# A decoder layer on eight cores: tail split by tokens, normalisation finish on two chunks per instruction, tanh gates, fifteen shared weight units, and a new instruction order

## Chip, cores and metric

The kernel runs on one Trainium2 chip, on 8 cores. Every core runs the same program on its own sequence, without talking to the others. The metric is the time of the slowest core, in microseconds (us). Each run lists the span of every core; the time is about 1.5 us more than the slowest span.

Some executions fall into a slower state: the cores of one die, or of both, show a lower granted clock and the time grows, in these runs to between 1601 and 1876 us. Only fast runs are compared below, and every time quoted is a median of fast runs. A ratio is the mean time of one kernel's fast runs over that of the other's fast runs of the same rounds, so it is not quite the ratio of the medians that are quoted.

## The reference, cut to what matters

```python
# one layer; d_model 1024, d_ff 2816; 2064 prompt tokens + 16 single-token samples per core
x = x + 0.5 * rmsnorm(swiglu(rmsnorm(x, g1a), Wg1, Wu1, Wd1), g1b)
h = rmsnorm(x, g2a); u = h @ W_in
yA = (A_b * dwconv3(A_c * A_x)) @ W_outA
#   RG-LRU:  r = sigmoid(x Wr + br);  i = sigmoid(x Wi + bi)
#            log_a = -8 r softplus(-lambda);  a = exp(log_a)
#            h_t = a_t h_{t-1} + sqrt(1 - a_t^2) * (i_t * x_t)
yB = (gelu(B_gate) * rglru(dwconv4(B_x))) @ W_outB
x = x + rmsnorm((sigmoid(gA) * yA + sigmoid(gB) * yB) @ W_o, g2b)
x = x + 0.5 * rmsnorm(swiglu(rmsnorm(x, g3a), Wg2, Wu2, Wd2), g3b)
```

## The kernel before

A core's 2080 tokens are cut into five streams of 414 to 418 columns, and one matmul works on the columns of one stream. The weights of the layer are cut into 117 units, mostly of 512 KB in bf16. A ring of ten slots (`wring`) holds units on the chip. Streams 0 and 1 form group 0 and use each unit together; streams 2, 3 and 4 are groups 1, 2 and 3. Group 0 reads the f32 weights (`wall`) with a cast on the way and writes a bf16 copy (`wsc`), which the later groups read. So during group 0, roughly the first 700 us, a core moves the most bytes for each matmul.

`JOIN` says for how many units stream 2 joins group 0 at the start, so that a unit serves three streams and is not fetched again:

```python
GROUPS = [[0, 1], [2], [3], [4]]
NW = 10          # slots of the weight ring
JOIN = 7
...
for u in range(JOIN if g == 1 else 0, NUNITS):
    w = head[u] if g == 0 and u < HEAD else at(g, u, "weights", None, issue_unit, g, u)
    ...
    for i in members:
        work(STREAMS[i], g, u, w)
    if g == 0 and u < JOIN:
        shared.append((u, w))          # stream 2 works on these too
```

The order of the instructions on each engine is not the order of the program text. A planner runs when the kernel is built. It simulates all engines and the DMA queues with its own durations, and at each step it gives an engine the ready operation with the best priority. The priorities come from tables of numbers (`LAGS`, `STARTS`, `ENDS`, `CLASSES`) that an earlier search found for this program. On the chip each engine then follows its fixed list and waits on semaphores. First, an operation that the planner thinks is late sits late in the list, whether or not it is late on the chip. Second, any edit can move the whole order.

```python
CAST_BW = 265e3                     # the planner's DMA figures before
COPY_BW = 400e3
DMA_CAP = (0.72, 0.95)
HW_SHARE = (0.43, 0.22)
DMA_LAT = 2.4
...
lo = min(c[0] for c in cands)
pick = min((c for c in cands if c[0] <= lo + PRI_EPS), key=lambda c: (c[1], c[2]))
```

The helpers `act`, `tt`, `stt` and `scan` record one ScalarE (ACT) or VectorE (DVE) operation each. The recurrent gate of one 128-channel block took nine ACT passes, all `Exp` and `Ln`:

```python
act(r, pzr, AF.Exp, scale=-1.0, bias=dcol(0, j));  act(b, pzi, AF.Exp, scale=-1.0, bias=dcol(1, j))
act(r, r, AF.Ln, bias=1.0);                        act(r, r, AF.Exp, scale=-1.0)
act(a, r, AF.Exp, scale=dcol(2, j));               act(r, r, AF.Exp, scale=dcol(5, j))
act(r, r, AF.Ln, bias=1.0, scale=-1.0);            act(b, b, AF.Ln, bias=1.0)
stt(r, r, 0.5, b, ALU.mult, ALU.subtract);         act(r, r, AF.Exp)
tt(cb, r, cb, ALU.mult);                           scan(b, a, cb, CAR[:, j:j + 1], ...)
```
(Lengths and dependency lists are cut in this excerpt.)

The finish of a normalisation is a multiply and an add per 128-row chunk, eight chunks. For the last stream nothing is left to hide them, and every two chunks are stored:

```python
for oc in range(KC):                                   # KC = 8
    yv = O32[s][:, oc * m:(oc + 1) * m]
    tt(tv[0:m], y32[s][:, oc, 0:m], rv[0:m], ALU.mult, ...)
    tt(yv, xs_view(st, oc, o, n), tv[0:m], ALU.add, ...)
    if st.last and (oc + 1) % 2 == 0:
        events.append(store_y(st, oc - 1, oc + 1))     # one contiguous piece per partition
```

## Time and profile before

| | before |
|---|---|
| time of the four fast runs beside the changed kernel | median 1564.96 us (1563.51 to 1565.91) |
| spans of the eight cores in the profiled run | 1557.1 to 1563.7 us, mean 1561.6 |
| TensorE (PE) busy on the slowest core | 1532.3 us |
| last matmul to end of span, all cores | 13.8 to 14.2 us |

The page of the profile, on the slowest core (core 0): the span, the busy time of each engine with the number of instructions, and the group of ACT table loads (busy time, mean ns of one, and the idle time before them with its main releaser).

```profile
span 1563.7 us, 27199 instructions; the slowest of 8 cores (1557.1 to 1563.7 us)
...
PE 1532.3 (98%) x8771; PEld 847.6 (54%) x8771; DVE 813.1 (52%) x1535; ACT 771.8 (49%) x1367; POOL 247.7 (16%) x470
...
L676 ACT ACT_TABLE_LOAD x84 | 107.8, 1283 | 28.9 <-PE P L662 19.2
```

PE is the bound. A gain must come from its start, its stalls or what follows its last matmul.

The view of waits for PE between 30 and 1535 us: what PE waited for, us in total, how often, the longest.

```profile
PE P L662 <- DVE qp L680: 3.9, 2, 2.8
PE P L662 <- DVE xs L704: 2.6, 2, 2.2
PE P L662 <- DMA wring<-wsc: 1.9, 2, 1.0
...
```

With a line of 0.7 us that is left out, the waits sum to 9.1 us in 1505 us. Two are long: 2.8 us for the norm of stream 2 near 80 us, and 2.2 us near 1233 us.

The view by windows (core 0): the window and its length, then busy us and instructions of PE, weight load, DVE, ACT and POOL, then granted clock, DMA share and GB/s.

```profile
60.00:80.00 20.00, 17.39 (x99) 9.32 (x96) 7.46 (x14) 6.62 (x14) 2.21 (x5) 1.00 0.70 158
80.00:100.00 20.00, 19.79 (x103) 10.63 (x104) 8.63 (x16) 6.75 (x10) 0.79 (x2) 0.91 0.75 187
300.00:320.00 20.00, 18.94 (x107) 10.20 (x106) 18.85 (x34) 17.01 (x33) 2.14 (x4) 1.00 0.69 162
...
700.00:720.00 20.00, 20.00 (x117) 11.14 (x115) 4.09 (x7) 4.07 (x8) 2.11 (x4) 1.00 0.92 170
1220.00:1240.00 20.00, 17.79 (x92) 9.15 (x91) 15.35 (x43) 14.88 (x28) 3.17 (x6) 0.91 0.53 171
```

A full window holds about 115 matmuls. The windows at 60, 80, 300 and 1220 us are short of that. After the two long waits the mean granted clock is 0.91: in finer windows it is 0.50 for about 3.4 us after each wait and 1.00 otherwise, so such a wait costs some ten matmuls more than its own length. At 300 us DVE (18.85 of 20 us) and ACT (17.01) are nearly full as well: this is the mixer of group 0, where the two are almost as scarce as PE.

The end of the span, from the timeline (start, length, engine, operation; in brackets the idle time before it and its releaser), and then the DMA view from 1549 us on, with the median us from issue to landing at the end of the second line:

```profile
1549.56 0.34 PE L662 MATMUL P<-qp,ones 128*128 128x414 bf16 x1 [0.58 <-ACT qp L676]
...
1551.27 0.59 DVE L680 TENSOR_TENSOR fp<-hy,fp 128x414 f32<-128x414 f32 x1 [5.01 <-ACT fp L676]
...
1560.32 0.59 DVE L680 TENSOR_TENSOR big<-xs,fp 128x414 f32<-128x414 f32 x1
```

```profile
DMA packets 576, 1.70 MB, mean 113 GB/s; under 512 B 64, under 2 KB 64, under 8 KB 576
...
yout<-big SPq DMA_DIRECT2D x4, 414.0 KB, 2.5
```

After PE's last matmul, sixteen DVE operations of 0.59 us run one after another, and 2.8 us after the last of them the span ends. Of the 576 packets, 512 are pieces of 3312 bytes (two chunks of 414 floats); each 414 KB store lands in 2.5 us.

### The profile page before, as it was taken

To read this page: it belongs to the slowest core of one execution; us is meant where nothing else is said; L and a number is where in the kernel's file an instruction comes from. 1 tells how busy PE (TensorE), PEld (TensorE's weight loads), DVE (VectorE), ACT (ScalarE), POOL (GpSimd) and SP (SyncE) were. 2 spreads that over 40 slices of the span, in tenths; PEclk is the share of its full clock that TensorE was granted. 3 is DMA by queue.
4 is the path that set the end of the run, shared out by engine and by line. 5 is a ranking of instruction groups with operands and counts; after the bars stand their busy time and mean duration, and the time that the engine had idled before them with its cause. 6 is when DMAs were issued, how large, how long until landed. Compare 5 with 4: busy or idle time off the path is not lost.

```text
span 1563.7 us, 27199 instructions; the slowest of 8 cores (1557.1 to 1563.7 us)
## 1 busy us (share of the span) xinstructions
PE 1532.3 (98%) x8771; PEld 847.6 (54%) x8771; DVE 813.1 (52%) x1535; ACT 771.8 (49%) x1367; POOL 247.7 (16%) x470
## 2 busy tenths in 40 slices
PE   8999999999999999999999999999999999999996
PEld 5555555555555555555555555555555555555553
DVE  3232108988787467722127452356567887661143
ACT  3221136788877567411154332446575678451222
POOL 1001111011111111011111122222221111112220
PEclk9999999999999999999999999999999999999998
DMA  9889767766877775898766776655575555545653
GB/s 192 227 193 205 155 159 179 200 146 190 203 162 191 201 201 145 200 203 188 180 178 189 249 247 202 198 181 172 183 254 202 163 174 186 205 170 181 199 185 106
DMA packets 81002, 294.88 MB, mean 189 GB/s; under 512 B 9696, under 2 KB 9824, under 8 KB 80864
## 3 DMA queue, kind: packets, MB, share of 16 engines
q0 software_dynamic: 60704, 223.12, 56.2%
q1 hardware_dynamic: 20160, 70.02, 11.9%
q8 instruction: 74, 1.21, 0.3%
q14 instruction: 64, 0.52, 0.1%
HBM read 284.76 MB, written 64.45 MB: 223 GB/s over the span
## 4 chain that ended last, share of the span: by engine, by line
PE 93%; DVE 3%; DMA 2%; issue 1%; ACT 1%; DVEq 0%; POOL 0%; SPq 0%; ACTq 0%; POOLq 0%
PE P L662 93%; DMA xs<-xin 1%; DMA wring<-wsc 1%; DVE fp L694 1%; DVE fp L680 1%; ACT fp L676 0%; DVE big L680 0%; ACT L676 0%; DVE xs L704 0%; DVE fp L699 0%; DVE fp L688 0%; DVEq L1143 0%; DVE qp L680 0%; ACT qp L676 0%; DVE xs L680 0%
## 5 line engine op out<-in xcount | busy, mean ns | idle before, releaser
L662 PE MATMUL P<-hy,wring 128*128 128x414 bf16 (+4 forms) x6080 | 1101.3, 339 | 5.7 <-DVE xs L704 2.2
L662 PEld LDWEIGHTS P<-hy,wring 128*128 128x128 bf16 x6080 | 591.0, 97 | 487.8 <-issue 14.4
L676 ACT ACTIVATE fp<-P 128x414 f32<-128x414 f32 (+4 forms) x529 | 267.7, 516 | 625.1 <-PE P L662 613.2
L662 PE MATMUL P<-big,wring 128*128 128x414 bf16 (+3 forms) x2400 | 442.8, 338 | 0.3 <-DVE xs L704 0.3
L680 DVE TENSOR_TENSOR big<-P,fp 128x414 bf16<-128x414 f32 (+3 forms) x260 | 151.2, 588 | 403.7 <-PE P L662 379.6
L662 PEld LDWEIGHTS P<-big,wring 128*128 128x128 bf16 x2400 | 233.2, 97 | 189.3 <-issue 1.0
L734 POOL DMA_DIRECT2D wring<-wsc x344 | 182.9, 532 | 802.5 <-PE P L662 786.1
L680 DVE TENSOR_TENSOR fp<-fp 128x414 f32<-128x414 f32 (+3 forms) x215 | 122.5, 572 | 131.2 <-ACT fp L676 124.3
L734 POOL DMA_DIRECT2D wring<-wall x117 | 62.0, 533 | 470.8 <-PE P L662 446.5
L676 ACT ACTIVATE fp<-fp 128x418 f32<-128x418 f32 (+2 forms) x230 | 121.1, 546 | 13.3 <-DVE fp L694 4.0
L676 ACT ACT_TABLE_LOAD x84 | 107.8, 1283 | 28.9 <-PE P L662 19.2
L694 DVE SCALAR_TENSOR_TENSOR fp<-P,par_sb,fp 128x418 f32<-128x418 f32 (+3 forms) x120 | 77.4, 646 | 24.9 <-ACT fp L676 16.9
L694 DVE SCALAR_TENSOR_TENSOR hy<-xs,par_sb,fp 128x414 bf16<-128x414 f32 (+3 forms) x120 | 69.1, 646 | 21.0 <-ACT fp L676 21.0
L694 DVE SCALAR_TENSOR_TENSOR fp<-fp,P 128x414 f32<-128x414 f32 (+3 forms) x80 | 45.4, 580 | 51.6 <-PE P L662 47.5
L676 ACT ACTIVATE fp<-xs 128x414 f32<-128x414 f32 (+3 forms) x104 | 55.1, 545 | 28.2 <-DVE xs L680 27.9
L694 DVE SCALAR_TENSOR_TENSOR fp<-fp,par_sb 128x402 f32<-128x402 f32 (+4 forms) x80 | 51.5, 644 | 7.2
L680 DVE TENSOR_TENSOR fp<-hy,fp 128x414 f32<-128x414 f32 (+3 forms) x80 | 46.7, 584 | 15.6 <-ACT fp L676 15.6
L676 ACT ACTIVATE fp<-fp,dpar 128x418 f32<-128x418 f32 (+2 forms) x80 | 51.1, 639 | 7.2 <-DVE fp L694 1.7
L676 ACT ACTIVATE hy<-P,dpar 128x414 f32<-128x414 f32 (+3 forms) x80 | 48.6, 607 | 7.5 <-ACT fp L676 0.7
L680 DVE TENSOR_TENSOR xs<-xs,fp 128x414 f32<-128x414 f32 (+3 forms) x80 | 47.1, 588 | 6.3 <-DVE fp L680 0.8
L676 ACT ACTIVATE fp<-P,dpar 128x418 f32<-128x418 f32 (+2 forms) x80 | 44.5, 604 | 10.6 <-PE P L662 8.9
L699 DVE TENSOR_TENSOR_SCAN fp<-fp,CAR 128x418 f32<-128x418 f32 (+3 forms) x40 | 43.1, 1076 | 3.8
(44 smaller groups left out, 379.4 us busy)
## 6 DMA issues: line engine op xcount, KB each, us to landing
wring<-wsc POOLq DMA_DIRECT2D x244, 512.0 KB, 4.7
wring<-wall POOLq DMA_DIRECT2D x83, 512.0 KB, 8.2
wsc<-wring SPq DMA_DIRECT2D x83, 512.0 KB, 7.0
wring<-wsc POOLq DMA_DIRECT2D x96, 352.0 KB, 4.1
wring<-wall POOLq DMA_DIRECT2D x32, 352.0 KB, 6.8
wsc<-wring SPq DMA_DIRECT2D x32, 352.0 KB, 5.6
xs<-xin SPq DMA_DIRECT2D x4, 828.0 KB, 7.5
xs<-xin SPq DMA_DIRECT2D x4, 418.0 KB, 6.4
```

Source lines behind the costliest of these rows:

```text
L662: ins = e.matmul(o, ev(lhs_list[k]), ev(rhs_list[k]), start=(start and k == 0), stop=(stop and k == nk - 1))
L676: return S.op("act", lambda e: e.activation(out=ev(out), in_=ev(in_), func=func, **kw), reads, writes, dur, tbl=TBL.get(func), prio=prio)
L680: return S.op("dve", lambda e: e.tensor_tensor(out=ev(out), in0=ev(in0), in1=ev(in1), op=op), reads, writes, 0.153 + n / 960.0, prio=prio)
L694: return S.op("dve", lambda e: e.scalar_tensor_tensor(out=ev(out), in0=ev(in0), scalar=scalar, in1=ev(in1), op0=op0, op1=op1), reads, writ ...
L699: return S.op("dve", lambda e: e.tensor_tensor_scan(out=ev(out), data0=ev(d0), data1=ev(d1), initial=init, op0=ALU.mult, op1=ALU.add), rea ...
L734: S.dma("pool", lambda e: e.dma_start(out=v[0:n](), in_=rows(src, off, n)), [R_xs(STREAMS[0], 3)] if g == 0 else [("wsc", u)], [v, ("wl", ...
```

## The change

The intent, in five parts:

1. **Tail.** The last two output chunks (6 and 7) of the last stream are computed for the first 207 tokens, then for the other 207. The finish of the first half can run under the matmuls of the second. One multiply spans four chunks. The sum is written in place in `xs` and stored from there.
2. **Finish on two chunks.** Elsewhere one DVE operation handles two chunks, the norm's factor being broadcast.
3. **Tanh gates.** `sigmoid(z) = (1 + tanh(z/2)) / 2` takes six ACT passes for nine.
4. **JOIN 15 for 7**, a different first load of x, weights that wait only for the first piece of x, the squares of stream 0 shared between ACT and DVE, an early table load.
5. **A new order**: new DMA figures in the planner, and all priority tables found anew for it.

The diff, cut to its core (the tables, some 130 lines of numbers on each side, and the plumbing are left out):

```diff
-XSTEP = [2, 4, 4, 4, 4]
+XSTEP = [4, 4, 4, 4, 4]
-JOIN = 7
+JOIN = 15
+TAIL_OC = 6
+TAIL_A = 207
 ... LAGS, STARTS, ENDS, CLASSES: all numbers replaced
-CAST_BW = 265e3
-COPY_BW = 400e3
-INPUT_BW = 320e3
-DMA_CAP = (0.72, 0.95)
-HW_SHARE = (0.43, 0.22)
-DMA_LAT = 2.4
+BEGIN = 1.1
+DMA_RATE = 21.5e3
+HW_TURN = 0.82
+DMA_LAT = 2.25
 ...
-        o.xfer = nbytes / (bw or (CAST_BW if cast else COPY_BW))
+        o.xfer = 8 * (nbytes / 128 / DMA_RATE + (stall if stall is not None else 0.085 if cast else 0.055))
 ...
 def post_norm(st, acc, o, src32, src_res):
-            for oc in range(KC):
-                tt(tv[0:m], src32[s][:, oc, 0:m], rv[0:m], ALU.mult, m, ...)
-                tt(xs_view(st, oc, o, n), xs_view(st, oc, o, n), tv[0:m], ALU.add, m, ...)
+            for oc in range(0, KC, 2):
+                tt(src, src, spread(rv[0:m], 2), ALU.mult, 2 * m, res + [rv], res)
+                tt(dst, dst, src, ALU.add, 2 * m, res + dres, dres)
 ...
+        def last_norm(st, acc, a, b):
+            xv = XS[s][:, 0:KC * n].rearrange("p (k t) -> p k t", k=KC)
+            for k0, nk, steps in ((0, 4, 1), (4, 4, 2)):
+                tt(src, src, spread(rv[0:m], nk), ALU.mult, nk * m, ...)
+                for k1 in range(k0, k0 + nk, nk // steps):
+                    yv = xv[:, k1:k2, o + a:o + b]
+                    tt(yv, yv, y32[s][:, k1:k2, a:b], ALU.add, (k2 - k1) * m, ...)
+                    dst = yout[:, base:base + (k2 - k1) * m].rearrange("p (k t) -> p k t", t=m)
+                    events.append(S.dma("sp", lambda e, dst=dst, yv=yv: e.dma_start(out=dst, in_=yv), ...))
 ...
-            act(r, pzr, AF.Exp, scale=-1.0, bias=dcol(0, j));  ... nine passes, shown above
+            act(r[0:n], pzr[0:n], AF.Tanh, ..., scale=0.5, bias=dcol(0, j), psum=True)
+            act(b[0:n], pzi[0:n], AF.Tanh, ..., scale=0.5, bias=dcol(1, j), psum=True)
+            act(a[0:n], r[0:n], AF.Exp, ..., scale=dcol(5, j), bias=dcol(5, j))
+            act(r[0:n], r[0:n], AF.Exp, ..., scale=dcol(2, j), bias=dcol(2, j))
             act(r[0:n], r[0:n], AF.Ln, ..., bias=1.0, scale=-1.0)
-            stt(r[0:n], r[0:n], 0.5, b[0:n], ALU.mult, ALU.subtract, n, [r, b], [r])
-            act(r[0:n], r[0:n], AF.Exp, n, [r], [r])
+            act(r[0:n], r[0:n], AF.Exp, ..., bias=cst[:, 1:2], scale=0.5)
+            stt(cb[0:n], b[0:n], 1.0, cb[0:n], ALU.add, ALU.mult, n, [b, cb], [cb])
```

## The prediction

> **What bounds the kernel now.** TensorE. The page shows PE busy 1532 of 1563.7 us; nearly every 20 us window from 100 to 1540 us is fully busy with about 115 matmuls. The change keeps the useful matmuls: 8771 less 166 warm-up ones are 8605, about 414 columns wide. The Trainium skill (TensorE: Matmul & The Clock Gate, Back-to-back issue gap) states N/2.4 + 2.5 ns when warm, 175 ns here; the trace agrees (176 to 177, stalls included). That is about 1507 us of streaming (estimate) that stays. The other 57 us are all there is to win:
> - start: by 29 us only about 33 useful matmuls are done, some 23 us lost. The chain of waits there is loads of xs; DMA share 0.83 and 1.01 in the first two windows.
> - stalls: at 80 us PE waits 2.83 us for the third stream's norm, then clock 0.91: the two windows hold 99 and 103 matmuls, 5 us lost. At 1233 us it waits 2.2 us, the window holds 92: 4 us. At 304, 860-880 and 1080-1100 about 1.3 us each.
> - tail: PE ends at 1549.9, the span at 1563.7: 13.8 us, of which sixteen DVE ops take 9.6 and the last store 2.8.
>
> **What changes.**
> 1. Tail. Output chunks 6 and 7 are split by tokens; the first half's finish runs under the second half's matmuls, and one op spans four chunks. After PE remain two multiplies and one add of 828 columns at about 1.0 us, two adds at 0.6: 4.2 us for 9.6. Shorter ACT ops and a smaller last store save 1 us. 88 short matmuls at about 97 ns (weight loads of the trace) for 44 at 175 cost 0.9 us. Net -5, all critical.
> 2. Two-run finish elsewhere: sixteen DVE ops of 0.59 us become eight of about 1.02, 1.2 us less per finish, little of it critical (DVE is 18 of 20 us busy in the mixer, 270-390 us).
> 3. Tanh gates: nine ACT passes per block become six, 3 x 0.55 x 40 = 66 us. But Ln now alternates with Tanh, and the Trainium skill (ScalarE: Activation LUTs, Table sets) puts them in different sets. A load takes 1283 ns in this trace (x84); up to 80 more are possible, I expect 30 to 60 (40 to 75 us). ACT comes out even, off PE's path except in the mixer.
> 4. JOIN 15: eight fewer weight units fetched (4 MB of 295), three streams' work per early weight, so DMA gets ahead and the stall at 80 us can go. The start stays: the bytes before the third weight unit (29 us) do. Early table load and two-piece x: -1 us.
> 5. A new order, tuned on a new DMA model: should remove half of the 13 us of stalls, may add some.
>
> **Sum.** -5 tail, -1 start, -7 stalls: 1552 us, range 1545 to 1560. Over 2% faster (below 1533) would need nearly all stalls and part of the DMA-bound start; chances 0.02 faster, 0.97 same, 0.01 slower.
>
> **What would show it.** Last matmul to end 8 to 9 us; windows 60-100 back to 115 matmuls; start unchanged within 2 us; activations down by about 120, table loads up by 30 to 60, ACT busy within 30 us; DVE down 15 to 20 us; PE's waits after 30 us under 8 us.
>
> **What would make it wrong.** Table switching that makes ACT late in the mixer and stalls PE; the new order starving the weight ring when group 1 begins; later x loads overtaking weights at the start; broadcast ops slower than 1.0 us per 828 columns.

## The result, and the profile after

| | before | after |
|---|---|---|
| time, median of four fast runs | 1564.96 us (1563.51 to 1565.91) | 1567.19 us (1566.96 to 1571.65) |
| ratio after/before, 95% interval | | 1.0022 (1.0002 to 1.0041) |
| spans of the cores, profiled run: slowest / mean / fastest | 1563.7 / 1561.6 / 1557.1 | 1565.4 / 1561.0 / 1554.6 |
| last matmul, mean of the cores | 1547.7 | 1546.2 |
| last matmul to end, mean of the cores | 13.9 | 14.8 |

The class "within 2%" was right. The value was not: 1552 was predicted, with a range that ended at 1560. The changed kernel is not faster; if anything it is 0.2% slower.

The page of the profile after (core 7, the slowest):

```profile
span 1565.4 us, 26856 instructions; the slowest of 8 cores (1554.6 to 1565.4 us)
...
PE 1531.3 (98%) x8817; PEld 849.7 (54%) x8817; DVE 804.1 (51%) x1422; ACT 748.6 (48%) x1268; POOL 243.4 (16%) x462
...
L675 ACT ACT_TABLE_LOAD x102 | 130.9, 1283 | 27.2 <-PE P L661 22.3
...
L679 DVE TENSOR_TENSOR hy<-hy,fp 128x828 f32<-128x828 f32 (+3 forms) x40 | 40.6, 1016 | 13.0 <-ACT fp L675 13.0
```

ACT and DVE do less work: ACT 748.6 us for 771.8 (117 activations fewer, 18 table loads more), DVE 804.1 for 813.1. A paired operation of 828 columns takes 1016 ns where two of 414 took about 590 each. The parts did what they should for their engines. But PE is the bound, and its own account matters.

The waits of PE after, 30 to 1535 us on core 7; smaller lines are left out. All nine sum to 10.8 us, for 9.1 before:

```profile
PE P L661 <- DMA wring<-wall: 2.3, 3, 1.0
PE P L661 <- DVE CAR L703: 2.1, 1, 2.1
PE P L661 <- ACT fp L675: 1.8, 4, 0.6
...
```

The two long waits of before are gone and there are new ones, of which the first kind is new on this core: waits for cast weights. The same windows as before, and three that became interesting (core 7):

```profile
60.00:80.00 20.00, 20.00 (x115) 10.96 (x113) 12.33 (x22) 10.08 (x18) 1.05 (x2) 1.00 0.92 240
80.00:100.00 20.00, 20.00 (x115) 11.08 (x114) 4.15 (x7) 3.63 (x7) 1.58 (x3) 1.00 0.41 80
300.00:320.00 20.00, 17.85 (x101) 9.47 (x100) 17.24 (x30) 16.14 (x26) 2.11 (x4) 1.00 1.03 218
340.00:360.00 20.00, 18.84 (x105) 9.90 (x105) 18.23 (x33) 18.38 (x30) 0.54 (x1) 1.00 0.06 20
700.00:720.00 20.00, 18.95 (x111) 10.43 (x109) 4.09 (x7) 4.11 (x8) 1.81 (x4) 1.00 0.96 193
1180.00:1200.00 20.00, 17.26 (x96) 8.73 (x95) 18.89 (x35) 16.50 (x29) 1.58 (x3) 1.00 0.32 106
1220.00:1240.00 20.00, 20.00 (x116) 11.05 (x115) 17.62 (x46) 15.62 (x25) 4.76 (x9) 1.00 0.68 215
```

The stall at 80 us is gone (99 + 103 became 115 + 115). The one at 1233 us is gone too, but 1180 to 1200 us holds 96 matmuls. In the mixer, 300 us got worse (101 for 107). At 340 us the DMA engines nearly rest (share 0.06, where before they were at 0.48), and at 700 us they are at 0.96 while PE misses six matmuls. The timeline of the weight queue in the stretch before that last window shows the rest once more:

```profile
686.95 0.53 POOL L734 DMA_DIRECT2D wring<-wall  x1 [27.79 <-PE P L661]
```

For 27.79 us the queue waited until PE freed a ring slot; then many units had to come at once.

To add the stretches up, this table gives the matmuls done in each window, as the mean of the eight cores (from the view by windows for every core), and the difference in us at 0.174 us each. Warm-up matmuls (166) and useful ones are counted alike in both kernels.

| window, us | before | after | difference, us |
|---|---|---|---|
| 0 to 30 (start) | 214.4 | 220.2 | -1.0 |
| 60 to 100 (stream 2 joins) | 203.0 | 228.2 | -4.4 |
| 100 to 260 | 904.0 | 901.2 | +0.5 |
| 260 to 400 (mixer of group 0) | 782.2 | 753.8 | +5.0 |
| 700 to 800 (group 1 begins) | 574.5 | 570.6 | +0.7 |
| 800 to 1100 | 1698.2 | 1712.4 | -2.5 |
| the other windows to 1400 | 3574.7 | 3573.5 | +0.2 |

So on the mean core the stalls after 30 us changed by only -0.5 us: what was cured at 80 us and after 800 us came back in the mixer of group 0. From 800 to 1100 us every core of before waited for `wring<-wsc`, the bf16 copies of the weights (0.2 to 2.7 us), and no core does so after. The old order had late weights too, in another place.

The tail after, from the timeline and the DMA view of core 7:

```profile
1548.99 0.25 PE L661 MATMUL P<-qp,ones 128*128 128x207 bf16 x1 [0.50 <-ACT qp L675]
...
1549.66 1.95 DVE L679 TENSOR_TENSOR hy<-hy,fp 128x828 f32<-128x828 f32 x2
...
1553.77 2.09 DVE L679 TENSOR_TENSOR xs<-xs,hy 128x414 f32<-128x414 f32 x4
```

```profile
DMA packets 2145, 1.70 MB, mean 100 GB/s; under 512 B 96, under 2 KB 2144, under 8 KB 2144
...
q1 hardware_dynamic: 2144, 1.70, 83.2%
...
yout<-xs SPq DMA_DIRECT2D x2, 414.0 KB, 7.9
yout<-xs SPq DMA_DIRECT2D x4, 207.0 KB, 8.8
```

DVE ends at 1555.9, which is 6.6 us after the last matmul instead of 11.0. That is most of the saving the change was after: before, DVE stood idle for 1.4 us after the last matmul and then worked for 9.6; after, it is idle for 0.4 and works for 6.2. One multiply and two adds of the first half, about 2.0 us, are still among these 6.2. But the same 1.70 MB now goes out as 2048 packets of 828 bytes and some 100 others. The DMA engines are full (83% of the stretch for this queue), and stores that took 2.5 us take 7.9 and 8.8. From the last DVE operation to the end there are 6.0 to 10.2 us on the eight cores, where there were 2.8 to 3.1. The drain gives back the whole saving.

The drain also differs by core. Where two neighbouring cores end their matmuls far apart (cores 4 and 5, 8.8 us apart) it is 6.0 us on both. Where they end close together (0 and 1, 4.3 us; 6 and 7, 4.0 us) it is 9.1 to 10.2; cores 2 and 3, 7.5 us apart, lie between (7.8 and 6.7). The rates in the DMA views of cores 6 and 7 (1540 to 1566 us in 40 slices of 0.65 us) fit a sharing by neighbours:

```profile
GB/s 0 0 0 0 0 0 0 0 0 0 178 310 177 0 6 338 308 196 106 102 103 84 76 88 126 111 108 103 82 18 1 0 0 0 0 0 0 0 0 0
...
GB/s 0 0 0 0 0 0 0 0 0 0 0 0 0 0 0 0 110 239 84 90 104 103 103 111 111 101 90 96 105 117 121 162 200 220 203 125 27 0 0 0
```

Core 6 moves over 300 GB/s and falls to about 100 when the stores of core 7 begin; core 7 rises from about 100 to 200 when those of core 6 end. The other pair that overlaps for long, 0 and 1, does the same. Each core's times count from its own first instruction, so this takes it that a pair starts together; no run tested it.

Last, the spans of the cores after:

```profile
...
core 4: 1554.6 us, clock 0.996
core 5: 1563.4 us, clock 0.994
...
core 7: 1565.4 us, clock 0.995
```

The cores lie 10.8 us apart, where they lay 6.6 apart before. The metric is the slowest of them. Cores 3, 5 and 7, the three slowest, are also those on which PE waits for cast weights after 60 us: 2.3, 4.0 and 2.3 us. Before, no core had more than 0.2 us of these. And they are the three that start slowest: in the first 30 us they do 213, 207 and 211 matmuls, the other five 217 to 234.

### The profile page after: what moved, and what is told of

It reads as the page before. It is cut to its first block, busy times and chain, and to the rows that moved or that the text cites. A ratio compares the mean times of both kernels' runs of the same rounds, so it can differ in the third digit from the quotient of the medians.

```text
span 1565.4 us, 26856 instructions; the slowest of 8 cores (1554.6 to 1565.4 us)
## 1 busy us (share of the span) xinstructions
PE 1531.3 (98%) x8817; PEld 849.7 (54%) x8817; DVE 804.1 (51%) x1422; ACT 748.6 (48%) x1268; POOL 243.4 (16%) x462
## 3 DMA queue, kind: packets, MB, share of 16 engines
q1 hardware_dynamic: 21440, 70.02, 12.5%
## 4 chain that ended last, share of the span: by engine, by line
PE 89%; DMA 4%; DVE 3%; ACT 2%; issue 2%; DVEq 0%; POOL 0%; ACTq 0%; POOLq 0%; SPq 0%
PE P L661 89%; DMA wring<-wall 2%; ACT fp L675 1%; DMA xs<-xin 1%; DVE fp L693 1%; DMA wsc<-wring 1%; ACT L675 0%; DVE fp L679 0%; DVE hy L679 0%; DVE xs L679 0%; DVE fp L698 0%; ACT qp L675 0%; DVE big L679 0%; ACT big L675 0%; DVE xs L703 0%
## 5 line engine op out<-in xcount | busy, mean ns | idle before, releaser
L661 PE MATMUL P<-hy,wring 128*128 128x414 bf16 (+5 forms) x6080 | 1097.9, 338 | 9.5 <-DVE CAR L703 2.1
L661 PE MATMUL P<-big,wring 128*128 128x414 bf16 (+4 forms) x2444 | 442.6, 335 | 0.9 <-DMA wring<-wall 0.5
L734 POOL DMA_DIRECT2D wring<-wsc x336 | 178.7, 532 | 797.9 <-PE P L661 774.2
L679 DVE TENSOR_TENSOR fp<-fp 128x414 f32<-128x414 f32 (+4 forms) x215 | 123.0, 573 | 115.8 <-ACT fp L675 105.7
L675 ACT ACTIVATE fp<-xs 128x414 f32<-128x414 f32 (+3 forms) x104 | 50.8, 541 | 28.8 <-DVE xs L679 19.5
L675 ACT ACTIVATE fp<-fp,dpar 128x418 f32<-128x418 f32 (+2 forms) x80 | 58.4, 731 | 7.8 <-DVE hy L679 3.7
L675 ACT ACTIVATE hy<-P,dpar 128x414 f32<-128x414 f32 (+4 forms) x82 | 49.1, 598 | 7.3
L679 DVE TENSOR_TENSOR big<-big,fp 128x414 bf16<-128x414 bf16 (+7 forms) x60 | 42.4, 726 | 12.2 <-ACT fp L675 11.5
L679 DVE TENSOR_TENSOR hy<-hy,fp 128x828 f32<-128x828 f32 (+3 forms) x40 | 40.6, 1016 | 13.0 <-ACT fp L675 13.0
L675 ACT ACTIVATE fp<-P,par_sb 128x418 f32<-128x418 f32 (+2 forms) x40 | 27.9, 697 | 30.4 <-PE P L661 26.5
```

The source lines that it names most:

```text
L661: ins = e.matmul(o, ev(lhs_list[k]), ev(rhs_list[k]), start=(start and k == 0), stop=(stop and k == nk - 1))
L675: return S.op("act", lambda e: e.activation(out=ev(out), in_=ev(in_), func=func, **kw), reads, writes, dur, tbl=TBL.get(func), prio=prio)
L679: return S.op("dve", lambda e: e.tensor_tensor(out=ev(out), in0=ev(in0), in1=ev(in1), op=op), reads, writes, 0.153 + n / 960.0, prio=prio)
L734: S.dma("pool", lambda e: e.dma_start(out=v[0:n](), in_=rows(src, off, n)), [R_xs(STREAMS[0], 0)] if g == 0 else [("wsc", u)], [v, ("wl", ...
```

## Experiments

The theory after reading the two traces had three terms. (a) The in-place tail pays for its short rows in the drain. (b) The mixer of group 0 is slower, because of table switching in the gates, or of the paired operations, or of late weights, or of the order alone. (c) The new order leaves DMA less slack, so cores that start late run into late weights, and the slowest core gains nothing. The rivals are in the list of (b), and for the cure at 80 us: JOIN 15, or the planner's new DMA figures.

All runs below gave correct results unless stated. Each call had its own chip and its own runs of the kernel before.

### e1_flat: the last adds write contiguous memory, order planned anew

```diff
-                    yv = xv[:, k1:k2, o + a:o + b]
-                    tt(yv, yv, y32[s][:, k1:k2, a:b], ALU.add, (k2 - k1) * m,
-                       [("half", a, k0)] + [R_xs(st, k) for k in range(k1, k2)], [("o32", a, k1)])
+                    flat = XS[0][:, KC * a + k1 * m:KC * a + k2 * m]
+                    tt(flat.rearrange("p (k t) -> p k t", t=m), xv[:, k1:k2, o + a:o + b], y32[s][:, k1:k2, a:b], ALU.add,
+                       (k2 - k1) * m, [("half", a, k0)] + [R_xs(st, k) for k in range(k1, k2)],
+                       [("o32", a, k1)] + [("xs", 0, k) for k in range(KC)])
```

> The changed kernel with the last finish adding into a contiguous buffer, so that a store's piece per partition is 1656 or 3312 bytes in place of runs of 828 bytes; nothing else. Theory (the 828-byte runs make the last stores slow): the stores at the end move over 200 GB/s in place of about 100, last matmul to end falls from about 15 us (median of the cores) to 9 to 10, time 1560 to 1562, faster than both. Rival (the stores are slow for another reason: issue by SyncE, or all cores writing at once): tail stays within 1 us of 15, time stays at 1567.

Measured: 1566.13 us beside 1565.70; ratio 1.0007 (0.9993 to 1.0021). The expected gain was not there. The drain did fall, to 2.6 to 4.0 us. But the dependencies that I had added for the buffer put the first half's first add behind the second half's multiply in the DVE list: DVE now ended 8.6 us after the last matmul rather than 6.6, and the tail was 11.2 to 12.5 us. So the drain was confirmed as a cost, but its worth was not yet measured cleanly; e2_flat does that.

### p1_noln: no table switching for the gates' `Ln`

In the order of e1_flat, held fixed, the gates' one `Ln` is emitted as `Exp`. Its output is wrong, which doesn't matter for the time.

```diff
-            act(r[0:n], r[0:n], AF.Ln, n, [r] + DP, [r], bias=1.0, scale=-1.0)
+            act(r[0:n], r[0:n], AF.Ln, n, [r] + DP, [r], bias=1.0, scale=-1.0, emit=AF.Exp)
```

> As e1_flat, but the Ln between the gates' Tanh and Exp is emitted as Exp (wrong numbers on purpose), with every engine's order held: the gates then need no table switch. Theory (the new waits of TensorE in the first mixer come from the order of work): table loads fall by 20 to 40, the matmul count of 260-400 us stays near 755, time within 2 us of e1_flat. Rival (table switching makes ACT late and TensorE with it): the count rises to 775 or more, time 4 to 6 us below e1_flat.

Measured: 1568.11 us; ratio 1.0017 (1.0001 to 1.0033). The page has 27 table loads fewer than with the `Ln` (102):

```profile
L675 ACT ACT_TABLE_LOAD x75 | 96.2, 1283 | 30.8 <-PE P L661 26.5
```

ACT is 36 us less busy (712.4 for 747.9), in 260 to 400 us the table loads fall from 12 to 6 (core 0; before has 7), and that window still holds 748 to 760 matmuls (745 to 757 in e1_flat). Table switching, which my prediction named first among the things that could go wrong, is not the cause of the slower mixer.

### p2_oneset: sigmoid gates of `Exp` and `Ln` in the new order

In the order of e1_flat, held fixed, the gates are computed as before, all from `Exp` and `Ln`, in ten passes (the extra ones sit directly before the pass that they belong to).

```diff
-            act(r[0:n], pzr[0:n], AF.Tanh, n, [pzr] + DP, [r], scale=0.5, bias=dcol(0, j), psum=True)
-            act(b[0:n], pzi[0:n], AF.Tanh, n, [pzi] + DP, [b, turn], scale=0.5, bias=dcol(1, j), psum=True)
+            act(r[0:n], pzr[0:n], AF.Tanh, ..., scale=-1.0, bias=dcol(0, j), psum=True, emit=AF.Exp)
+            ob = act(b[0:n], pzi[0:n], AF.Tanh, ..., scale=-1.0, bias=dcol(1, j), psum=True, emit=AF.Exp)
+            S.ops[ob].pre = [S.ops[ob].fn, more(b, AF.Ln, bias=1.0)]
+            S.ops[ob].fn = more(b, AF.Exp, scale=-1.0)
+            S.ops[oa].pre = [more(r, AF.Ln, bias=1.0), more(r, AF.Exp, scale=-1.0)]
```

> As e1_flat, with sigmoid gates from Exp and Ln only (one table set) in the slots of the tanh gates: ten ACT passes per block in place of six, no table switch within the gates, every engine's order held. Theory (fewer ACT passes did help, since ACT is 15 to 17.6 of 20 us busy in the mixer): ACT busy up by 50 to 70 us, TensorE's waits in the mixers grow, time 5 to 25 us above e1_flat. Rival (tanh gates are the cause of the loss): time below e1_flat by 3 us or more.

Measured: 1646.67 us; ratio 1.0524 (1.0504 to 1.0544).

ACT is busy 845.1 us, 97 more than in e1_flat, and the time grows by 81 us. The lost matmuls lie where the gates run: on the mean core 260 to 400 us has 669 matmuls (750 in e1_flat), 400 to 700 us 1503 (1712), 1100 to 1400 us 1526 (1687). The loss was far larger than I had expected. In a fixed order that counts on six passes, almost every pass added there turns into a wait of PE. It doesn't say that tanh gates are worth 81 us: the old order, tuned for nine passes, loses nothing like that. It says that the new order needs them.

### p3_single: finish with one chunk per operation in the new order

In the order of e1_flat, held fixed, each paired operation is issued as two of one chunk.

```diff
-                tt(src, src, spread(rv[0:m], 2), ALU.mult, 2 * m, res + [rv], res)
-                tt(dst, dst, src, ALU.add, 2 * m, res + dres, dres)
+                x = tt(s1, s1, rv[0:m], ALU.mult, 2 * m, res + [rv], res)
+                S.ops[x].pre = [lambda e, s0=s0: e.tensor_tensor(out=s0, in0=s0, in1=ev(rv[0:m]), op=ALU.mult)]
+                x = tt(d1, d1, s1, ALU.add, 2 * m, res + dres, dres)
+                S.ops[x].pre = [lambda e, d0=d0, s0=s0: e.tensor_tensor(out=d0, in0=d0, in1=s0, op=ALU.add)]
```

> As e1_flat, with the finish of all but the last one done a chunk per instruction as before, two instructions in the slot of one, every order held. Theory (the paired finish is a small gain): DVE busy up by about 17 us, time 0 to 2 us above e1_flat. Rival (the long paired ops hold DVE too long and cause the new waits): time 2 us or more below e1_flat.

Measured: 1577.44 us; ratio 1.0076 (1.0062 to 1.0091), so about 11 us slower than e1_flat. DVE is 15.4 us busier (820.5 for 805.1), and PE has fewer matmuls in 100 to 260 us (872 to 893; e1_flat 895 to 905), 260 to 400 us (734 to 745; 745 to 757) and 400 to 700 us (1688 to 1697; 1704 to 1717). I had called little of this critical. It is critical in the stretches where DVE is nearly full. The pairs help; they are not what slows the mixer.

### e2_flat: the contiguous tail with the order of the changed kernel unchanged

The same edit as e1_flat without the extra dependencies, checked to leave the order on every engine exactly as in the changed kernel. Only the destination of the last adds, and the stores' source, differ.

```diff
-                       [("o32", a, k1)] + [("xs", 0, k) for k in range(KC)])
+                       [("o32", a, k1)])
```
(relative to e1_flat)

> As e1_flat without the extra order on VectorE that e1_flat brought (its first add waited behind the second half's multiply, and VectorE ended 8.6 us after the last matmul in place of 6.6): every engine's order is that of the changed kernel, only the place that the last adds write is another. Theory (stores of 828-byte runs are the whole of what the tail lost): last matmul to end 9 to 9.6 us on all cores (after: 12.6 to 16.8), drain after the last VectorE op 2.6 to 3.1 us (after: 6 to 10), time 1562 to 1565. Rival (the tail is off the path of the slowest core): time stays at 1566 to 1567.

The DMA view of its end:

```profile
yout<-xs SPq DMA_DIRECT2D x2, 414.0 KB, 2.6
yout<-xs SPq DMA_DIRECT2D x4, 207.0 KB, 2.2
```

Against the changed kernel the drain fell from 6.0 to 10.2 us to 2.7 to 3.5, and the tail from 12.6 to 16.8 us to 9.3 to 10.1 on every core. That is the tail the prediction had (8 to 9), one us longer, with the first half's last three operations still after PE's end. Term (a) is shown: the stores in rows of 828 bytes cost the tail its gain, and nothing else had to be changed to get it back. The mean span of the cores is 1556.9 us, 4.1 less than after.

The time, however, is 1565.60 us beside 1565.69; ratio 1.0004 (0.999 to 1.0018). The mean core gained and the slowest did not. On that core (7) the last matmul ends at 1554.7, later than on any core of before, and its waits are:

```profile
PE P L661 <- DMA wring<-wall: 5.8, 9, 2.1
PE P L661 <- ACT fp L675: 2.4, 4, 1.2
...
```

Cores 0, 5 and 7, the slowest three (1560.6, 1560.0 and 1564.1 us), waited 3.0, 4.6 and 5.8 us for cast weights after 60 us.

### e2_half and before_half: half the bytes of every weight unit

In e2_flat and in the kernel before, every weight unit is fetched and written back at half its size, in the same order; the matmuls read the same half twice. Their outputs are wrong, which doesn't matter for the times. If late weights make the slow cores slow, they should catch up here.

```diff
+            c = n // 256 * 128
-            S.dma("pool", lambda e: e.dma_start(out=v[0:n](), in_=rows(src, off, n)),
+            S.dma("pool", lambda e: e.dma_start(out=v[0:c](), in_=rows(src, off, c)),
+            off %= HALF[v]
```

> e2_flat with half the bytes of every weight unit: the first half is fetched, written back and used twice (wrong numbers on purpose); every engine's order, every matmul and every other op is the same. Theory (the slowest core of the changed kernel is the one of each neighbouring pair that gets its weights late; the new order leaves less slack for that in the first group, so what it wins on the fast cores is lost on the slow ones): no wait of TensorE for wring<-wall is left, counts of 100-260 and 700-800 us equal on all cores (904, 575), spread of the cores after the start under 3 us (e2_flat: 11 to 15 us), and the slowest core at or below the fastest of e2_flat (1551 us), time 1545 to 1553. Rival (the slow cores are slow for another reason, such as clock): spread stays at 10 us or more.

> The same cut in the kernel before. Theory: it gains less than e2_flat does, since no wait for wring<-wall was there to remove (5 to 10 us, most of it at the start): time 1555 to 1560, so that with light DMA the new order with the mended tail is 5 us or more below the old one. Rival (the new order is no better even with weights always there): the two are within 2 us.

Measured, fast runs: e2_half 1559.32 and 1557.29 us (its other two were slow), ratio to before 0.9946 (0.9928 to 0.9964); before_half 1562.36 us (1560.63 to 1562.79), ratio 0.997 (0.9956 to 0.9983). The waits of PE on core 7 of e2_half begin so, and no line of them names DMA:

```profile
PE P L661 <- DVE CAR L703: 2.1, 1, 2.1
PE P L661 <- DVE hy L693: 1.5, 4, 0.8
...
```

With half the bytes the new order gains 0.58% (0.9946 over e2_flat's 1.0004, about 9 us) and the old one 0.30% (about 5 us). The difference, some 4 us, would be what the new order loses to bytes beyond what the old one does. The three intervals leave about 4 us of doubt on it (estimate), and e2_half has only two fast runs, so by itself it only just supports term (c); the waits and the counts below are the firmer evidence. In the old order the gain lies mostly in 800 to 1100 us, where every core now does 1712 matmuls (1692 to 1709 before), and not at the start, where I had expected it. Three more facts come out of it. The counts of 100 to 260 us (904) and 700 to 800 us (575 to 576) become equal on all cores, so the shortfalls in those windows were late weights. The mixer window stays at 748 to 758 matmuls, so its loss is not late weights. And the time did not fall as far as I had expected: the slowest core ends at 1557.8 us (expected 1551), the cores lie 7.3 us apart (expected under 3). They still start unequally (188 to 238 matmuls in the first 30 us), and those that start with fewest end last. The loads of x were not halved; that they are the reason is not shown.

### before_tail and before_tail2: the tail alone, in the kernel before

The kernel before, with its own tables, planner and JOIN, gets the split tail with the contiguous store of e2_flat. before_tail2 also tells the planner to take the last six units of the last group in chunk order:

```diff
+for _t, _p in ((STARTS[3], 40.0), (ENDS[3], 40.0)):
+    _b = max(_t[101:111])
+    for _u in range(111, NUNITS):
+        _t[_u] = _b + _p * (_u - 110)
```

> The kernel before with the split finish of the last stream alone, stored from the contiguous buffer; old gates, old JOIN, old tables. Theory (the tail is worth about 4 us by itself, wherever the rest of the order comes from): last matmul to end 9 to 9.6 us in place of 13.9, about 0.9 us more TensorE work, time 1560 to 1562 (before: 1564 to 1566). Rival (the new order is needed for it): 1564 or more.

> before_tail with one more edit to the tables: the last six down-projection units of the last group in the order of their chunks, so that the first half's finish really runs under the second half's matmuls (in before_tail the table put chunk 5 last and the first half's finish began after TensorE's end; last matmul to end stayed at 12.4 to 13.4). Theory: last matmul to end 9.3 to 9.7 us, TensorE's end as before plus 0.9, so 3 to 3.5 us below before: 1561 to 1563. Rival (TensorE's end or the slowest core moves with it, as in e2_flat): 1565 to 1566.

before_tail: 1564.34 us; ratio 0.9998 (0.9981 to 1.0014), tails of 12.4 to 13.4 us. Its timeline (core 2) shows why:

```profile
1551.38 1.02 DVE L682 TENSOR_TENSOR hy<-hy,fp 128x828 f32<-128x828 f32 x1 [2.11 <-ACT fp L678]
```

This is the finish of the *first* half, and PE had ended at 1550.21. The old tables put chunk 5 at the very end, after the split chunks, and the first half's sum needs every chunk. The split hid nothing.

before_tail2: 1563.27 us (1560.59 to 1564.68); ratio 0.9972 (0.996 to 0.9985), tails of 8.4 to 9.5 us. So the tail as intended is worth about 5 us in a program whose order is touched only in its last units, and the time gained 0.28%, close to it. This version beats both kernels.

### before_newdma: the planner's new DMA figures alone

The kernel before with JOIN 7 and its own tables, and only the new DMA figures in the planner.

```diff
-CAST_BW = 265e3
-COPY_BW = 400e3
-INPUT_BW = 320e3
-DMA_CAP = (0.72, 0.95)
-HW_SHARE = (0.43, 0.22)
-DMA_LAT = 2.4
+BEGIN = 1.1
+DMA_RATE = 21.5e3
+HW_TURN = 0.82
+DMA_LAT = 2.25
-        o.issue = 0.6 if eng == "pool" else 0.1
+        o.issue = 0.55 if eng == "pool" else 0.43
 ... (the rules that use these figures are cut)
```

> The kernel before with only the planner's new figures for DMA: what it emits differs in order alone. Theory (the wait at 80 us came from the planner expecting the third stream's x too late, so that its norm stood too late in the fixed order; JOIN is not what cures it): the matmul count of 60-100 us rises from 202 to about 228, and other waits of TensorE appear in the mixers at 300 and near 480 to 525 us, as tables that were tuned for another plan no longer fit; time 1570 to 1582. Rival (only JOIN 15 cures the wait at 80 us): the count stays near 202.

Measured: 1587.92 us; ratio 1.0153 (1.0134 to 1.0171), worse than I had expected. But the windows (core 6) show the cure of the stall at 80 us, without JOIN 15:

```profile
60.00:80.00 20.00, 20.00 (x114) 10.82 (x113) 8.16 (x16) 9.44 (x17) 2.12 (x4) 1.00 0.76 157
80.00:100.00 20.00, 20.00 (x115) 11.03 (x114) 8.04 (x15) 3.98 (x8) 2.12 (x4) 1.00 0.58 149
260.00:400.00 140.00, 134.75 (x752) 73.18 (x751) 118.43 (x212) 112.46 (x205) 16.60 (x32) 0.99 0.69 174
```

So the order from the new DMA figures lets PE run through 60 to 100 us without the sharing of units. (Half as much is lost before 60 us: on the mean core 30 to 60 us holds 163 matmuls for 171, with a new wait of 1.2 us near 38 us. By 100 us this order is 12 matmuls ahead of before, where the changed kernel is 31 ahead.) The same figures with the old tables lose 30 matmuls in 260 to 400 us, the size of loss that the changed kernel has there, with old gates and single operations, and 94 more in 400 to 700 us. Another order can lose the mixer by itself.

### oldtabs_flat: the tables of before on the new operations

e1_flat with `LAGS`, `STARTS`, `ENDS` and `CLASSES` of the kernel before. One line of many:

```diff
-           "weights": (0, -753.31),
+           "weights": (0, -188.30),
```

> e1_flat with the priority tables of the kernel before; gates, finish, JOIN 15 and tail are the new ones. Theory (order tables and code are tuned to each other, the new operations alone bring nothing): time 1572 to 1584, the loss showing as waits of TensorE in windows between 260 and 700 us. Rival (the new operations gain and only the new tables lose): time below 1562.

Measured: 1582.73 us; ratio 1.0111 (1.0095 to 1.0128). 260 to 400 us holds about 710 matmuls, 400 to 700 us about 1677. Operations and tables were tuned to each other; neither half of the change can be judged by simply taking out the other.

### tuned1: the operations of e2_flat, the order moved

The tables of e2_flat are moved by a search on the program's own planner. A candidate is judged by the planned time with its DMA figures as they are and also with DMA 3% and 6% slower, so that an order without slack is not chosen. Nothing but numbers in the tables changes, for instance:

```diff
-CLASSES = {"first": (0, -295.27),
+CLASSES = {"first": (0, -412.87),
...
-           "pre": (1, -374.93),
+           "pre": (1, -843.76),
```

> e2_flat with its priority tables moved by a search that plays each order on the program's own planner also with DMA 3 and 6 per cent slower, and keeps those orders that lose little then; operations, JOIN and tail are those of e2_flat. Theory (the changed kernel's order leaves too little slack for late weights in the first group, and the slowest core pays for it): waits of TensorE for wring<-wall after 60 us under 1.5 us on every core (e2_flat: up to 5.8), spread of the core spans 10 us or less (e2_flat: 10 to 15), fastest core 1549 to 1552 as before, time 1559 to 1562, below before and e2_flat. Rival (the slack is not what holds the slowest core): the time stays at 1565 to 1567.

Measured: 1559.41 us (1558.48 to 1560.92, six runs) beside 1565.27; ratio 0.9967 (0.9954 to 0.998). The slowest core of its profiled run and the fastest:

```profile
core 3: 1557.2 us, clock 0.996
...
core 6: 1551.8 us, clock 0.997
```

On the slowest core the wait for cast weights is

```profile
PE P L661 <- DMA wring<-wall: 0.5, 1, 0.5
```

and no core has more than that after 60 us. The operations are those of e2_flat, and the fastest core is where e2_flat's was (1551.3). The slow ones moved most: the slowest from 1564.1 to 1557.2. This agrees with term (c), but it is no isolated test, since the search moved the whole order: of about 22 matmuls that the mean core gains against e2_flat from 30 to 1400 us, 6 come in 1100 to 1400 us. It has the lowest time of the kernels with correct results, but its interval overlaps that of before_tail2, so the two can't be ranked. It still has long rests of the weight queue (27.7 us the longest): a rest does not by itself make a wait.

The tables of cores, from the profiled run of each kernel:

| kernel | last matmul, mean | tail, mean | mean core | slowest core | slowest less mean |
|---|---|---|---|---|---|
| before | 1547.7 | 13.9 | 1561.6 | 1563.7 | 2.1 |
| after | 1546.2 | 14.8 | 1561.0 | 1565.4 | 4.4 |
| e2_flat | 1547.4 | 9.5 | 1556.9 | 1564.1 | 7.2 |
| before_tail2 | 1549.1 | 8.8 | 1557.9 | 1563.0 | 5.1 |
| tuned1 | 1544.5 | 10.0 | 1554.5 | 1557.2 | 2.7 |

The last column moves by a few us from run to run (after: the slowest core was at 1565.4, 1565.5, 1565.8 and 1570.1 in its four fast runs), so it is read for its size only. Averaged over all fast runs, the slowest core less the mean is 3.0 us in the kernel before (32 runs), 5.3 after (4), 6.9 in e2_flat (5), 3.6 in before_tail2 (6), 3.4 in tuned1 (6), 2.4 in e2_half (2) and 2.8 in before_half (4).

## Why the prediction was wrong

The prediction added -5 (tail), -1 (start) and -7 (stalls) to -13 us. Measured was +2. On the mean core, the account from the tables above is:

| term | predicted | measured, mean core |
|---|---|---|
| tail | -5 | +0.9 |
| start | -1 | -1.0 |
| stalls after 30 us | -7 | -0.5 |
| slowest core against the mean | not in the sum | +2.3 |

The terms come from different views (counts of matmuls, ends, spans) and are not expected to add up to the last tenth.

**Step 1, the tail, "Net -5, all critical": this failed.** DVE ended 6.6 us after the last matmul instead of 11.0, a gain of 4.4. The ACT part of it was right: the idle time of DVE after the last matmul fell from 1.4 to 0.4 us. The DVE part, "4.2 us for 9.6", was right in kind and too small: 6.2 us remained, because one multiply and two adds of the first half (2.0 us) did not fit under the second half's matmuls. (The short matmuls cost less than feared: 89 ns each, not 97, so 88 of them add about 0.2 us and not 0.9.) The term that failed is "a smaller last store save[s] 1 us". The store was smaller but was cut into rows of 828 bytes, and from the last DVE operation to the end it took 6.0 to 10.2 us in place of 2.8 to 3.1. I read the destination of the adds in the diff and did not draw the conclusion for the descriptors. e2_flat, which changes only that, has the tail of 9.3 to 10.1 us, 4.4 us less than before; before_tail2, in another order, has 8.4 to 9.5.

**Steps 4 and 5, "-7 stalls": this failed too.** The stall at 80 us went away as predicted, worth 4.4 us. The reason given for it, JOIN 15, was not needed: the order from the planner's DMA figures does it with JOIN 7 (before_newdma), though that order loses half as much again before 60 us. JOIN 15 with the old figures was not run. From 800 to 1100 us another 2.5 us came, as the waits for bf16 copies went. The sentence "should remove half of the 13 us of stalls, may add some" counted the first half and left "some" at zero. What it added is 5.0 us in the mixer of group 0, and 1.2 us in the two windows where weights come late. PE's waits after 30 us, predicted under 8 us, are 7.8 to 8.9 on five cores and 10.8 to 13.0 on cores 3, 5 and 7. The stall at 1233 us was replaced by one at 1180.

**The slowest core was not in the sum at all.** I read the trace of one core and took its gains for the metric. The new order has less slack for weights in group 0. The cores that start late wait for them, and these are the cores that set the time. In the kernel before, the late copies held up cores that started early too (2.7 us on cores 6 and 7, though 0.2 on core 1). e2_flat shows it best: in the profiled runs its mean core is 4.7 us faster than that of before and its slowest core 0.4 slower; over all fast runs of its call the two are 2.9 faster and 0.8 slower. Halving the bytes (e2_half) and an order chosen with slower DMA in mind (tuned1) both bring the slowest core down by some 6 to 7 us in the profiled runs, without moving the fastest by more than 1. The prediction had named "starving the weight ring when group 1 begins" as a danger. It did occur, at 700 us and in 100 to 260 us.

**What was right.** The bound: PE, with some 115 matmuls to a full 20 us. The Trainium skill (TensorE: Matmul & The Clock Gate, Back-to-back issue gap) gives N/2.4 + 2.5 ns as the warm gap of an isolated matmul. For 414 columns that is 175 ns (estimate), and full windows in both traces have 115 to 117 in 20 us, 171 to 174 ns. The same section says that this formula over-counts for a stream of weight loads and matmuls with many columns; these traces, which are such a stream, don't show that. The start (-1.0), though to hit it so closely was luck: on the mean core the four kernels that keep the old start do 205 to 214 matmuls in the first 30 us. ACT: 117 activations fewer, and its busy time within 30 us of before. (Six passes are not two thirds of nine, because two of the new ones take scale and bias from memory: the Trainium skill, ScalarE: Activation LUTs, What ACT_TABLE_LOAD costs, has about 93 ns for each such pointer operand, and the trace after agrees with 549, 643 and 733 ns for none, one and two on 418 columns.) The price of a paired operation, 1.02 us for 828 columns: the page has 1016 ns. DVE fell by 9 us, less than the 15 to 20 predicted.

**What was too large a worry.** Table loads rose by 18, not by 30 to 60. The Trainium skill (ScalarE: Activation LUTs, Table sets) puts `tanh` with `exp` in one set and `ln` with `exp` in another. That `tanh` beside `ln` costs loads agrees with p1_noln, where 27 loads go when the `Ln` goes. But the planner batches the passes of several blocks, and taking all these loads away changed nothing for PE.

**What stays open.** The 5.0 us that the new order loses in 260 to 400 us are not table switching (p1_noln), not the paired operations (p3_single makes it worse), not late weights (e2_half). Tanh gates and JOIN 15 were not taken out one by one with an order tuned for each, so the order of that stretch is what is left, by elimination and not by a test of its own. On the slowest core the waits there are 5.3 us in five kinds, the longest 2.1, against 1.5 before. They are nearly the same on all eight cores (4.7 us on six of them). In the wait of 2.1 us DVE is busy throughout. The copy of the scan's last column, which the profile names as what PE waited for, stands in DVE's list behind three operations that take 2.14 us (core 7):

```profile
315.92 2.14 DVE L693 SCALAR_TENSOR_TENSOR fp<-P,par_sb,fp 128x418 f32<-128x418 f32 x3
317.98 0.14 DVE L703 COPY CAR<-fp 128x1 f32<-128x1 f32 x1
```

On cores 2 and 6 the clock then fell to half for 3.4 us, which is why they have 748 matmuls in this stretch and most others 752 to 758. before_newdma shows that another order alone can lose as much there. Why the cores differ at the start is also open; in the first 30 us a core does between 204 and 234 matmuls, and in most neighbouring pairs one core is ahead and the other behind.

## What to carry to other kernels

When a store is made smaller to shorten a tail, count the bytes of each contiguous row, not only those of the store: here the sum ended 4.4 us earlier and the drain took up to 7 us more. When the metric is the slowest of several cores, predict the slowest: add up the slack for late data on the cores that start late, not only the stalls of the core in the profile. And in a program whose order is planned by a tuned table, a part that is taken out or put in alone is measured with somebody else's order; hold the order and change one thing, as e2_flat does, or say which order it was.

## What the Trainium skill lacked or had wrong

- **DMA: Bandwidth & Descriptors (Why small descriptors are slow).** The page gives a fixed cost of about 3 cycles for each packet on the internal bus beside one cycle for 32 bytes, and fixed descriptor metadata of 32 bytes. For rows of 828 bytes that is about 10% for the cycles and 4% for the metadata (estimates from that page). At the beginning of a drain the trace is near that: by its packet records a row of 828 bytes takes 38 to 40 ns and a piece of 3312 bytes 131 to 133 ns, so a byte in short rows costs 15 to 22% more. What the page doesn't have is what follows. After some 1250 rows a row takes mostly 45 to 80 ns on a core alone, and mostly 105 to 160 ns while the neighbour stores too. Pieces of 1656 bytes (e2_flat) stay at 69 to 75 ns and pieces of 3312 at 129 to 134. Why the short rows slow down later was not separated from their alignment.
- **HBM Reference (its opening lines).** It says that pairs of cores share this memory, but has no example of what that does to a tail. Here, with rows of 828 bytes, the four cores whose stores overlap their neighbour's for most of the drain moved 101 to 109 GB/s in that time (bytes over packet time, for 16 engines). Cores 4 and 5, which did not overlap, moved 226 to 249 GB/s over the drain. In the kernel before, with pieces of 3312 bytes, each core kept 401 to 408 GB/s beside a storing neighbour. This is one profiled run of each, on the assumption that a pair starts together, and it was not tested.
- **TensorE: Matmul & The Clock Gate (What's actually happening).** The page says that the clock falls after at least one idle window of about 3.4 us. In the kernel before, a single wait of 2.8 us near 80 us, with PE busy on both sides, was followed by about 3.4 us at half the clock (0.50; a mean of 0.91 in the 20 us window), and so was the wait of 2.2 us near 1233 us. In the changed kernel, 1180 to 1200 us had 2.7 us in sum without a busy PE and the clock stayed at 1.00; and after the wait of 2.1 us near 316 us, the same on all eight cores, it fell on cores 2 and 6 alone. So a wait shorter than the window can be enough; when it is, these runs don't say.
